# A streaming encoder step on one core: ties settled in a branch per tile, the sixteen rounds in a branch of their own, eleven gate tiles ahead of attention, and part of a convolution tile summed on VectorE

## The chip, the cores and the metric

The kernel runs on one core of a Trainium2 chip. The core has a matrix engine (TensorE, PE in the profile; PEld are its weight loads), VectorE (DVE), ScalarE (ACT), GpSimd (POOL) and a queue for DMA issues (SyncE, SP). Each engine works through its own instruction list in order and waits on semaphores for the others. The metric is the device time of one execution in microseconds (us), the median of several runs; lower is better.

## The reference

One layer of an encoder over 1024 prompt frames and 64 sample frames (1088 tokens, width 1024, float32). What the change touches is the selection of keys for attention and the causal convolution.

```
h = x + 0.5 * swiglu(rms(x));  u = rms(h);  z = u @ W_in
q, k, v, qi, ki, wi, conv_in, gate = split(z)
# indexer and selection
s     = einsum('bqhd,bsd->bqhs', qi, k_idx)
score = einsum('bqh,bqhs->bqs', wi, relu(s));  score = where(admissible, score, -inf)
_, sel = top_k(score, top)            # top = 256 (prompt) or 48 (sample); the lower index wins a tie
attn  = attention of q over the selected keys only
# convolution branch
c  = ca * sigmoid(cb)
dc = depthwise_conv(c_pad, conv_w, width 31) + conv_b      # 512 channels
conv_out = silu(layernorm(dc)) @ conv_w_out
# merge
g_a, g_c = sigmoid(gate + b_gate)
h = h + (g_a * (attn @ attn_w_out) + g_c * conv_out) @ w_out
h = h + 0.5 * swiglu(rms(h));  y = rms(h)
```

The inputs are drawn from a fixed seed, so each execution sees the same scores. Frame t may read the keys up to the end of its chunk of 64. Selection is needed only where more keys are admissible than are kept: six prompt tiles of 128 rows with 384, 512, 640, 768, 896 and 1024 keys, and the sample tile of 64 rows with 192 keys. That makes 832 rows and 4416 key columns in all.

## The kernel before, in words

**Stages.** First feed-forward block (PE, to about 780 us); a middle part with the projections of u, rotary, indexer, selection, attention, convolution and merge (about 780 to 1775 us); second feed-forward block (to the end). Every float32 matmul is done as three passes (`mm3`, L136 to L138) on operands that are split into a high and a low part: ACT makes the high part (`whi`), POOL the low part (`wlo`, L119).

**The middle part in program order.** `conv_in(t)` projects u and makes the gated convolution input of channel tile t in DRAM (`d_c`). `conv(t, ...)` loads it (`ci`), sums 31 shifted copies and stores the result (`d_dc`). For tiles 0, 1 and 2 ACT multiplies by the tap (`pd`, L679) and POOL adds (`ac`, L680), in two halves of 559 tokens; for tile 3 one DVE instruction a tap multiplies and adds (L665) in a PSUM bank, in three pieces. Then come rotary (`rope`, DVE), the indexer (matmuls into `lgi` PSUM banks, ACT relu, DVE weighting into the scores `Y`, L836/L838), the value projection, `conv(1)`, `conv(2)`, the query projection, and then the selection.

**The selection on DVE.** Scores are searched by bits. Fifteen rounds (L901) find the high 16 bits `hib` of each row's threshold. Then the eight largest low halves among the scores that share these high bits are taken (`top8`), the threshold's rank among them is `thr`, and if it is at most 7 the low half `lob` is read off; `nxt` becomes the difference to the next low half (L947). A mask is written to `bias` (L958: 0 for a kept key, a large negative number for others). If `nxt` is zero in any row (a tie, or a rank over 7, for which `lob` and `nxt` come out as zero), the flag `deepi` is set (L948 to L954), DVE loads it into a register (L961) and branches (L962). In that branch sixteen more rounds over all seven tiles (L973 to L983, the counting at L979) find the low half bit by bit, and then eight instructions a tile (L990 to L998) rank the tied keys and rewrite the mask of all seven tiles. The search's small arrays (`srch`, `sb_` in the code) lie in a PSUM bank of the pool `lgi`.

**After the selection.** Keys, values and queries of attention are loaded (`K`, `vt`, `qts`). The 16 gate tiles (`gates`, tanh of a projection of u, three chunks of 364, 362 and 362 tokens each, 24 matmuls a chunk) are split: the first `GPRE` = 10 run ahead of attention with the PSUM pool `ps4`; the rest are the first work of `background()`, which fills attention's gaps, in the pool `psf`, whose banks lie where `ps4` and `lgi` were. After the first ten, `cvs.close()`, `low.close()` and `ps_es.close()` free the convolution's and the search's memory, and attention's tiles (`pr`, `lg`, L1066 to L1083) are put there. `lg` scores queries against keys, L1069 adds the mask, and so on.

**What sets the order.** A scheduler orders each engine's instructions at build time, by priorities (`high_priority`) and its own estimates; at run time the lists are fixed. Nothing crosses a branch on DVE; the other engines have one plain jump there and no condition.

Of the kernel before, what the change touches and what calls it, by code (L numbers as in the profile page):

```python
# [54 lines left out]
CW = 31  # L55
# [12 lines left out]
STILES = [(128 * i, 128, 0, 128 * (i + 1), TOP_P) for i in range(2, 8)]  # L68
# [7 lines left out]
NT = len(STILES)  # L76
# [16 lines left out]
class Kern:  # L93
# [346 lines left out]
    def run(self):  # L440
        tc, nc, a = self.tc, self.nc, self.a
        PS = bass.MemoryType.PSUM
        with ExitStack() as top:
# [6 lines left out]
            d_c = dram.tile([4, P, 1148], F32, name="d_c")  # L450
            d_dc = dram.tile([4, P, 1118], F32, name="d_dc")
# [192 lines left out]
            lgi = self.pool(ps_es, "lgi", 4, space=PS)  # L644
# [7 lines left out]
            kp = self.pool(low, "topk", 1, side="right")  # L652
            Y = kp.tile([P, YCOLS], F32, name="Y")

            def conv(t, dve):
                x = "d" if dve else "p"
                if dve:
                    for s0, w in ((0, 374), (374, 372), (746, 372)):
                        ci = cvp_.tile([P, 589], F32, name="ci", tag="ci" + x)[:, :w + 30]
                        nc.sync.dma_start(ci, d_c[t, :, s0:s0 + w + 30])  # L660
                        ac = lgi.tile([P, 512], F32, name="acc", tag="lgi")[:, :w]
                        nc.scalar.activation(ac, ci[:, 0:w], AF.Identity, scale=par("convw", t * CW),
                                             bias=par("convb", t))
                        for j in range(1, CW):
                            nc.vector.scalar_tensor_tensor(ac, ci[:, j:j + w], par("convw", t * CW + j), ac,  # L665
                                                           op0=ALU.mult, op1=ALU.add)
                        co = cvp_.tile([P, 559], F32, name="ac", tag="ac" + x)[:, :w]
                        nc.scalar.activation(co, ac, AF.Copy)
                        nc.sync.dma_start(d_dc[t, :, s0:s0 + w], co)
                    return  # L670
                for s0 in (0, 559):
                    ci = cvp_.tile([P, 589], F32, name="ci", tag="ci" + x)
                    nc.sync.dma_start(ci, d_c[t, :, s0:s0 + 589])
                    ac = cvp_.tile([P, 559], F32, name="ac", tag="ac" + x)
                    nc.scalar.activation(ac, ci[:, 0:559], AF.Identity, scale=par("convw", t * CW),
                                         bias=par("convb", t))
                    for j in range(1, CW):
                        pd = cvp_.tile([P, 559], F32, name="pd", tag="pd", bufs=2)
                        nc.scalar.activation(pd, ci[:, j:j + 559], AF.Copy, scale=par("convw", t * CW + j))  # L679
                        nc.gpsimd.tensor_tensor(ac, ac, pd, op=ALU.add)  # L680
                    nc.sync.dma_start(d_dc[t, :, s0:s0 + 559], ac)

            def load_q(pool, src, t0, rows, qpool=None, qb=2, n=1280):

# [180 lines left out]
            conv(1, False)  # L865
            conv_in(2, ep)
            conv(2, False)

            rope_pairs(tb, d_q)
            tbs.close()  # L870
# [68 lines left out]
            def threshold():  # L939

                nc.vector.tensor_copy(mi0, hib)
                nc.vector.tensor_copy(mi1, lob)
                nc.vector.tensor_scalar(mi0, mi0, 16, None, op0=ALU.logical_shift_left)
                nc.vector.tensor_tensor(sth.bitcast(I32), mi0, mi1, op=ALU.bitwise_or)  # L944
# [4 lines left out]
            nc.vector.transpose(deep[:, 32:64], deep[:, 0:32])  # L949
            nc.vector.tensor_reduce(deep[:, 64:65], deep[:, 32:64], axis=AX.X, op=ALU.min)  # L950
            for q in range(1, 4):
                nc.vector.tensor_copy(deep[0:1, 64 + q:65 + q], deep[32 * q:32 * q + 1, 64:65])
            nc.vector.tensor_reduce(deep[0:1, 68:69], deep[0:1, 64:68], axis=AX.X, op=ALU.min)
            nc.vector.tensor_scalar(deepi, deep[0:1, 68:69], 0.5, None, op0=ALU.is_lt)  # L954
# [7 lines left out]
            with tc.If(more > 0):  # L962


                nc.vector.tensor_scalar(flag, hib, float(1 << 15), None, op0=ALU.is_lt)
                nc.vector.tensor_scalar(sgn, flag, 2.0, -1.0, op0=ALU.mult, op1=ALU.add)
                nc.vector.tensor_tensor(thr, ktop, lmk, op=ALU.subtract)
                nc.vector.tensor_tensor(thr, thr, flag, op=ALU.mult)
                nc.vector.tensor_tensor(thr, thr, lmk, op=ALU.add)
                nc.vector.memset(lob, 0.0)  # L970
                nc.vector.tensor_copy(low_, lob)
                for b in range(15, -1, -1):
                    nc.vector.tensor_scalar(lob, low_, float(1 << b), None, op0=ALU.add)  # L973
                    threshold()
                    nc.vector.tensor_tensor(cand, sth, sgn, op=ALU.mult)
                    for n in VT + (XT,):
                        rows, y0, L = rows_of(n)
                        c1 = slice(COL[n], COL[n] + 1)
                        nc.vector.scalar_tensor_tensor(spare(n), Y[:rows, y0:y0 + L], sgn[:rows, c1],  # L979
                                                       cand[:rows, c1].to_broadcast([rows, L]),  # L980
                                                       op0=ALU.mult, op1=ALU.is_ge, accum_out=cnt[:rows, c1])
                    nc.vector.tensor_tensor(flag, cnt, thr, op=ALU.is_ge)
                    nc.vector.scalar_tensor_tensor(low_, flag, float(1 << b), low_, op0=ALU.mult, op1=ALU.add)  # L983
                nc.vector.tensor_copy(lob, low_)
                threshold()
                for n in VT + (XT,):
                    rows, y0, L = rows_of(n)
                    c1 = slice(COL[n], COL[n] + 1)
                    y, b = Y[:rows, y0:y0 + L], spare(n)
                    nc.vector.tensor_scalar(b, y, sth[:rows, c1], 0.0, op0=ALU.is_le, op1=ALU.add,  # L990
                                            accum_out=cnt[:rows, c1])
                    nc.vector.tensor_scalar(need[:rows, c1], cnt[:rows, c1], float(STILES[n][4] - L), None, op0=ALU.add)
                    nc.vector.tensor_scalar(y, y, sth[:rows, c1], None, op0=ALU.is_equal)
                    nc.vector.tensor_tensor_scan(y, y, y, 0.0, op0=ALU.add, op1=ALU.bypass)
                    nc.vector.tensor_scalar(y, y, need[:rows, c1], -NEG, op0=ALU.min, op1=ALU.mult)
                    nc.vector.scalar_tensor_tensor(b[:, 0:1], b[:, 0:1], NEG, y[:, 0:1], op0=ALU.mult, op1=ALU.add)
                    nc.vector.tensor_tensor(y[:, 0:L - 1], y[:, 1:L], y[:, 0:L - 1], op=ALU.subtract)
                    nc.vector.scalar_tensor_tensor(b[:, 1:L], b[:, 1:L], NEG, y[:, 0:L - 1], op0=ALU.mult, op1=ALU.add)  # L998
# [504 lines left out]
```

## Time and profile before

| | us |
|---|---|
| median of 3 runs | 2552.09 (2544.73 to 2552.24) |
| profiled execution: its own time | 2549.7 |
| profiled execution: span from first to last instruction | 2547.9 |
| PE busy | 2316.0 (91%) |
| DVE busy | 1847.4 (73%) |
| POOL busy | 1435.6 (56%) |
| ACT busy | 1164.8 (46%) |
| mean granted TensorE clock | 0.959 |

The profiled execution is 1.8 us longer than its span, and 2.4 us shorter than the median of the runs. A row of a timeline gives start, duration, engine, line, operation, output<-inputs, shapes, number of merged instructions, and in brackets how long the engine had been idle and what ended that. Where several instructions are merged in one row, the duration is from the first start to the last end. Busy PE time is modelled from overlapping records; two consecutive starts give the true pace. `L979` is line 979 of the kernel before.

### The profile page before, as it was taken

Reading aid. Unit: us, or ns where it says so; the run is one execution under the profiler, and the core shown is the slowest. Engines: PE = TensorE matmul, PEld = TensorE weight load, DVE = VectorE, ACT = ScalarE, POOL = GpSimd, SP = SyncE. Lnnn points to the kernel's source line nnn. Section 1 sums busy time; section 2 is a strip of 40 time slices with the busy share of each in tenths; the row PEclk is TensorE's granted clock in tenths of the full one; section 3 lists DMA queues with packets and bytes.
Section 4 is the critical chain, followed back from the end, with each engine's and each line's share of the span. In section 5 each row is a group of like instructions: output and inputs, shape, how many; then the busy total and the mean of one; then the engine's idle time right before and its main releaser. Section 6 shows DMA issues by size and latency. Waiting matters only on the chain.

```text
span 2547.9 us, 44592 instructions
## 1 busy us (share of the span) xinstructions
PE 2316.0 (91%) x16762; PEld 2283.4 (90%) x16762; DVE 1847.4 (73%) x4138; ACT 1164.8 (46%) x2237; POOL 1435.6 (56%) x873
## 2 busy tenths in 40 slices
PE   7999999999999999993048989989999999999998
PEld 6999999999999999993048888979999999999998
DVE  7766678766673776899996788557776668767676
ACT  6433345443355568862014555444444345344343
POOL 5455566555466868796045345546555565555554
PEclk9999999999999999997569999989999999999999
DMA  5222323223234432331002245564222222323223
GB/s 181 109 96 96 108 100 118 84 92 108 91 114 137 138 118 87 124 125 46 0 23 68 85 154 164 185 218 144 100 100 92 84 100 84 105 105 118 90 93 110
DMA packets 130408, 273.46 MB, mean 107 GB/s; under 512 B 17936, under 2 KB 77200, under 8 KB 130192
## 3 DMA queue, kind: packets, MB, share of 16 engines
q1 hardware_dynamic: 130192, 270.61, 31.3%
q8 instruction: 132, 2.16, 0.3%
q14 instruction: 84, 0.69, 0.1%
HBM read 231.87 MB, written 38.75 MB: 106 GB/s over the span
## 4 chain that ended last, share of the span: by engine, by line
PE 71%; DVE 16%; DMA 4%; POOL 4%; issue 3%; ACT 2%; SPq 0%; DVEq 0%; ACTq 0%; POOLq 0%
PE ps L136 22%; PE ps L138 22%; PE ps L137 22%; DVE bias L979 4%; POOL ac L680 3%; DMA raw<-wf 1%; PE pt L1093 1%; DMA ga<-d_g 1%; DVE bias L901 1%; DVE ps L312 1%; DVE ga L1230 1%; PE ps L166 1%; DVE x L153 1%; DVE s L314 1%; DVE t L211 1%
## 5 line engine op out<-in xcount | busy, mean ns | idle before, releaser
L119 POOL TENSOR_TENSOR wlo<-raw,whi 128x1024 fp32r<-128x1024 f32 (+1 forms) x187 | 437.3, 2343 | 377.8 <-ACT whi L118 373.9
L136 PE MATMUL ps<-x,whi 128*128 128x272 f32 (+2 forms) x1544 | 484.5, 314 | 137.5 <-DVE sth L944 119.8
L136 PE MATMUL ps<-x,wp 128*128 128x272 f32 x1760 | 506.5, 289 | 3.2 <-ACT wp L152 3.2
L138 PE MATMUL ps<-x,wp 128*128 128x272 f32 x1760 | 503.6, 290 | 2.0 <-DVE wp L153 1.0
L137 PE MATMUL ps<-x,wp 128*128 128x272 f32 x1760 | 505.1, 288 | 0.0
L138 PE MATMUL ps<-x,wlo 128*128 128x272 f32 (+2 forms) x1544 | 481.9, 313 | 0.0
L136 PEld LDWEIGHTS ps<-x,whi 128*128 128x128 f32 x1544 | 294.4, 191 | 140.8 <-DVE sth L944 120.5
L137 PE MATMUL ps<-x,whi 128*128 128x272 f32 (+2 forms) x1334 | 413.7, 310 | 0.9 <-POOL x L153 0.9
L136 PE MATMUL ps<-gh,whi 128*128 128x272 f32 x1408 | 400.1, 289 | 5.6 <-DVE spare L284 3.5
L137 PE MATMUL ps<-gl,whi 128*128 128x272 f32 x1408 | 405.2, 289 | 0.0
L138 PE MATMUL ps<-gh,wlo 128*128 128x272 f32 x1408 | 404.2, 289 | 0.0
L680 POOL TENSOR_TENSOR ac<-ac,pd 128x559 f32<-128x559 f32 x180 | 287.0, 1595 | 157.7 <-ACT pd L679 132.3
L153 POOL TENSOR_TENSOR wlo<-raw,whi 128x1024 fp32r<-128x1024 f32 x88 | 221.4, 2517 | 256.2 <-ACT whi L152 256.2
L136 PEld LDWEIGHTS ps<-x,wp 128*128 128x128 f32 x1760 | 331.2, 188 | 4.2 <-ACT wp L152 4.0
L138 PEld LDWEIGHTS ps<-x,wp 128*128 128x128 f32 x1760 | 328.8, 188 | 3.9 <-DVE wp L153 2.7
L137 PEld LDWEIGHTS ps<-x,wp 128*128 128x128 f32 x1760 | 331.5, 188 | 0.0
L153 POOL TENSOR_TENSOR wp<-s,wp 128x512 fp32r<-128x512 f32 x176 | 256.6, 1458 | 103.3 <-ACT wp L152 103.3
L428 DVE SCALAR_TENSOR_TENSOR h<-ps,h 128x272 f32<-128x272 f32 x384 | 164.4, 438 | 186.9 <-PE ps L138 186.2
L138 PEld LDWEIGHTS ps<-x,wlo 128*128 128x128 f32 x1544 | 294.0, 191 | 1.2
L118 ACT ACTIVATE whi<-raw 128x1024 fp32r<-128x1024 f32 (+1 forms) x187 | 190.5, 1020 | 221.3 <-PE ps L137 110.3
L136 PEld LDWEIGHTS ps<-gh,whi 128*128 128x128 f32 x1408 | 263.5, 189 | 6.9 <-DVE spare L284 3.9
L138 PEld LDWEIGHTS ps<-gh,wlo 128*128 128x128 f32 x1408 | 266.3, 189 | 0.0
(264 smaller groups left out, 5035.6 us busy)
## 6 DMA issues: line engine op xcount, KB each, us to landing
raw<-wf SPq DMA_DIRECT2D x337, 512.0 KB, 3.3
raw<-wf SPq DMA_DIRECT2D x32, 384.0 KB, 3.0
d_g<-sg SPq DMA_DIRECT2D x32, 181.0 KB, 1.9
d_h<-h SPq DMA_DIRECT2D x2, 2176.0 KB, 10.5
y<-t SPq DMA_DIRECT2D x32, 136.0 KB, 1.9
raw<-d_q SPq DMA_DIRECT2D x32, 128.0 KB, 3.5
raw<-d_qi SPq DMA_DIRECT2D x24, 128.0 KB, 3.1
d_g<-sg SPq DMA_DIRECT2D x16, 182.0 KB, 3.3
```

What stands on the lines that cost most here:

```text
L118: nc.scalar.activation(hi[:, :n], raw[:, :n], AF.Copy)
L119: self.weng.tensor_tensor(lo[:, :n], raw[:, :n], hi[:, :n], op=ALU.subtract)
L136: t.matmul(out, wh, xh, start=first, stop=False)
L137: t.matmul(out, wh, xl, start=False, stop=False)
L138: t.matmul(out, wl, xh, start=False, stop=last)
L153: (eng or nc.vector).tensor_tensor(lo, x, hi, op=ALU.subtract)
L166: self.nc.tensor.matmul(ps[:, b * P:(b + 1) * P], x[:, t0:t0 + P], self.ones, start=i == 0, stop=i == len(tiles) - 1)
L211: self.nc.vector.scalar_tensor_tensor(x, h[:, k, t0:t0 + w], self.par[:, q:q + 1], r, op0=ALU.mult, op1=ALU.mult)
L312: nc.vector.tensor_tensor(s[2], a0, b0, op=ALU.subtract)
L428: nc.vector.scalar_tensor_tensor(x, p, 0.5, x, op0=ALU.mult, op1=ALU.add)
L680: nc.gpsimd.tensor_tensor(ac, ac, pd, op=ALU.add)
L979: nc.vector.scalar_tensor_tensor(spare(n), Y[:rows, y0:y0 + L], sgn[:rows, c1], cand[:rows, c1].to_broadcast([rows, L]), op0=ALU.mult, op1 ...
```

## The change

Four things are changed.

1. **Two branches where there was one.** In the outer branch DVE now computes one flag for each tile (a row of it is tied: `nxt` is zero) and one more flag `far` (a row's rank is over 7 and its eighth low half isn't zero), with a helper `flags()` that reduces over the partitions, and stores them in `tiei`. The sixteen rounds stand in a nested branch on `far`. If it isn't taken, the low half found before is used as it is.
2. **Ties in a branch per tile.** For each of the seven tiles DVE loads the tile's flag and branches over six instructions (before: eight, for every tile). The rank goes to an array `rk` of its own, and the mask that L962 (L958 before) has written is corrected by one instruction.
3. **`GPRE` is 11**: one more gate tile stands ahead of attention.
4. **Convolution tile 0 is split** at token 506: VectorE sums the first 506 tokens in a PSUM bank as tile 3 does, ACT and POOL the other 612 in one piece. Tile 3 keeps its three pieces, tiles 1 and 2 their two halves.

```diff
-GPRE = 10
+GPRE = 11
...
-            def conv(t, dve):
...
+            def conv(t, pieces):
+
+                for s0, w, dve in pieces:
+                    x = "d" if dve else "p"
+                    ci = cvp_.tile([P, 536 + 106 * (not dve)], F32, name="ci", tag="ci" + x)[:, :w + 30]
+                    nc.sync.dma_start(ci, d_c[t, :, s0:s0 + w + 30])
+                    co = cvp_.tile([P, 506 + 106 * (not dve)], F32, name="ac", tag="ac" + x)[:, :w]
+                    ac = lgi.tile([P, 512], F32, name="acc", tag="lgi")[:, :w] if dve else co
...
+                    for j in range(1, CW):
+                        if dve:
                             nc.vector.scalar_tensor_tensor(ac, ci[:, j:j + w], par("convw", t * CW + j), ac,
                                                            op0=ALU.mult, op1=ALU.add)
+                        else:
+                            pd = cvp_.tile([P, 612], F32, name="pd", tag="pd", bufs=2)[:, :w]
+                            nc.scalar.activation(pd, ci[:, j:j + w], AF.Copy, scale=par("convw", t * CW + j))
+                            nc.gpsimd.tensor_tensor(ac, ac, pd, op=ALU.add)
...
-            conv(0, False)
-            conv(3, True)
+            conv(0, ((0, 506, True), (506, 612, False)))
+            conv(3, ((0, 374, True), (374, 372, True), (746, 372, True)))
...
+            def flags(src, first, dst):
+
+                w = src.shape[1]
+                f = [deep[:, first + 32 * i:first + 32 * i + 32] for i in range(3)]
+                nc.vector.transpose(f[1], f[0])
+                nc.vector.tensor_reduce(f[2][:, 0:1], f[1], axis=AX.X, op=ALU.min)
+                for q in range(1, 4):
+                    nc.vector.tensor_copy(f[2][0:w, q:q + 1], f[2][32 * q:32 * q + w, 0:1])
+                nc.vector.tensor_reduce(f[0][0:w, 0:1], f[2][0:w, 0:4], axis=AX.X, op=ALU.min)
+                nc.vector.transpose(f[1][0:32, :], f[0][0:32, :])
+                nc.vector.tensor_scalar(dst, f[1][0:1, 0:w], 0.5, None, op0=ALU.is_lt)
...
             with tc.If(more > 0):
...
+                nc.vector.tensor_copy(deep[:, 0:NT], nxt)
+                nc.vector.tensor_scalar(flag, thr, 7.5, None, op0=ALU.is_ge)
+                nc.vector.tensor_tensor(flag, flag, top8[:, :, 7], op=ALU.mult)
+                nc.vector.tensor_reduce(deep[:, NT:NT + 1], flag, axis=AX.X, op=ALU.max)
+                nc.vector.tensor_scalar(deep[:, NT:NT + 1], deep[:, NT:NT + 1], -1.0, 1.0, op0=ALU.mult, op1=ALU.add)
+                flags(deep[:, 0:NT + 1], 0, tiei)
+                far = nc.vector.value_load(tiei[:, NT:NT + 1], min_val=0, max_val=1)
+                with tc.If(far > 0):
+
+                    nc.vector.memset(tiei, 1)
...
+                for n in (5, 6, 4, 3, 2, 1, 0):
                     rows, y0, L = rows_of(n)
...
+                    tied = nc.vector.value_load(tiei[:, c1], min_val=0, max_val=1)
+                    with tc.If(tied > 0):
+                        y, b = Y[:rows, y0:y0 + L], spare(n)
+                        nc.vector.tensor_scalar(y, y, sth[:rows, c1], 0.0, op0=ALU.is_equal, op1=ALU.add,
+                                                accum_out=need[:rows, c1])
+                        nc.vector.scalar_tensor_tensor(need[:rows, c1], cnt[:rows, c1], 1.0 / NEG, need[:rows, c1],
+                                                       op0=ALU.mult, op1=ALU.add)
+                        nc.vector.tensor_scalar(need[:rows, c1], need[:rows, c1], float(STILES[n][4] - L), None,
+                                                op0=ALU.add)
+                        nc.vector.tensor_tensor_scan(rk[:rows, :L], y, y, 0.0, op0=ALU.add, op1=ALU.bypass)
+                        nc.vector.scalar_tensor_tensor(y, rk[:rows, :L], need[:rows, c1], y,
+                                                       op0=ALU.is_gt, op1=ALU.mult)
+                        nc.vector.scalar_tensor_tensor(b, y, NEG, b, op0=ALU.mult, op1=ALU.add)
```

Where the sixteen rounds and the old tie code stood, the rounds are unchanged inside the nested branch, and end with a fresh mask (seven instructions like L958).

How the change moves instructions shows at three places. The first is PE's list at the step from the gate tiles that run ahead to attention: `ps` are gate chunks, `lg` attention's first scores, `x` and `u` parts of u, `whi`/`wlo` a gate tile's weights. Before:

```order
L138 MATMUL ps_14509<-x_9450,wlo_14449 128x362
L1066 MATMUL lg_14561<-kh0_13603,qt_13634 128x512
L1067 MATMUL lg_14561<-kl0_13604,qt_13634 128x512
L1066 MATMUL lg_14565<-kh0_13603,qt_13634 128x512
L1067 MATMUL lg_14565<-kl0_13604,qt_13634 128x512
L1066 MATMUL lg_14570<-kh0_13603,qt_13634 128x512
L1067 MATMUL lg_14570<-kl0_13604,qt_13634 128x512
L962 UNCONDITIONAL_BRANCH
L136 MATMUL ps_14636<-x_9443,whi_14631 128x364
L137 MATMUL ps_14636<-x_9451,whi_14631 128x364
```

And PE's list at the same place with the change (`ps_14631` is the last chunk of the eleventh gate tile):

```order
L136 MATMUL ps_14631<-x_9449,whi_14570 128x362
L966 UNCONDITIONAL_BRANCH
L137 MATMUL ps_14631<-u_9457,whi_14570 128x362
L138 MATMUL ps_14631<-x_9449,wlo_14571 128x362
L136 MATMUL ps_14631<-x_9450,whi_14570 128x362
L137 MATMUL ps_14631<-u_9457,whi_14570 128x362
L138 MATMUL ps_14631<-x_9450,wlo_14571 128x362
L1091 MATMUL lg_14683<-kh0_13635,qt_13666 128x512
L1092 MATMUL lg_14683<-kl0_13636,qt_13666 128x512
...
L1092 MATMUL lg_14692<-kl0_13636,qt_13666 128x512
L136 MATMUL ps_14758<-x_9443,whi_14753 128x364
```

The 72 matmuls of the eleventh gate tile now stand ahead of the first `lg`; behind the first six `lg` matmuls PE goes on with gate chunks in both, and meets the next `lg` matmul after 168 gate rows before and after 101 with the change.

The second place is DVE's list at the outer branch with the change, from the flag `deepi` on (before, `deepi` at L954 was followed by its load L961, the branch L962 and at once by L965, the first of the sixteen rounds' preparation):

```order
L955 TENSOR_SCALAR deepi<-srch 1x1
L965 TENSOR_LOAD deepi
L966 COMPARE_AND_BRANCH
L969 COPY srch<-nxt 128x7
...
L955 TENSOR_SCALAR tiei<-srch 1x8
L975 TENSOR_LOAD tiei
L976 COMPARE_AND_BRANCH
L978 MEMSET tiei 1x8
L979 TENSOR_SCALAR flag<-srch 128x7
```

And where the first of the seven tiles' branches stands, behind the nested branch:

```order
L1003 SCALAR_TENSOR_TENSOR bias,cnt<-Y,sth,negc 128x1024
L976 UNCONDITIONAL_BRANCH x2
L975 ISA x2
L1011 TENSOR_LOAD tiei
L1012 COMPARE_AND_BRANCH
L1014 TENSOR_SCALAR Y,need<-Y,sth 128x1024
L1016 SCALAR_TENSOR_TENSOR need<-cnt,need 128x1
L1020 SCALAR_TENSOR_TENSOR rk<-Y 128x1024
L1018 TENSOR_SCALAR need<-need 128x1
L1021 SCALAR_TENSOR_TENSOR Y<-rk,need,Y 128x1024
L1023 SCALAR_TENSOR_TENSOR bias<-Y,bias 128x1024
L1012 UNCONDITIONAL_BRANCH x2
```

Between the two pieces lie some 260 rows, the nested branch's, which DVE jumps over if `far` is not set; the last piece comes seven times, once a tile.

The third place is DVE's list at the convolution (`acc` is the PSUM bank, `sg` belongs to `conv_in(3)`, whose PSUM source `ps` PE is to reuse, `m0` and `m1` to rotary). Before and with the change:

```order
L623 SCALAR_TENSOR_TENSOR sg_10141<-sg_10141,ps_10195 128x364
L623 SCALAR_TENSOR_TENSOR sg_10168<-sg_10168,ps_10223 128x362
L665 SCALAR_TENSOR_TENSOR acc_10501<-ci_10499,par_72,acc_10501 128x374 x4
L623 SCALAR_TENSOR_TENSOR sg_10251<-sg_10251,ps_10278 128x362
L665 SCALAR_TENSOR_TENSOR acc_10501<-ci_10499,par_72,acc_10501 128x374 x4
L580 TENSOR_TENSOR m0_10696<-ps_10645,cos_10616 128x364
```

```order
L667 SCALAR_TENSOR_TENSOR acc_10312<-ci_10309,par_72,acc_10312 128x506 x14
L623 SCALAR_TENSOR_TENSOR sg_10141<-sg_10141,ps_10195 128x364
L667 SCALAR_TENSOR_TENSOR acc_10312<-ci_10309,par_72,acc_10312 128x506 x4
L623 SCALAR_TENSOR_TENSOR sg_10168<-sg_10168,ps_10223 128x362
L667 SCALAR_TENSOR_TENSOR acc_10312<-ci_10309,par_72,acc_10312 128x506 x9
L623 SCALAR_TENSOR_TENSOR sg_10251<-sg_10251,ps_10278 128x362
L667 SCALAR_TENSOR_TENSOR acc_10312<-ci_10309,par_72,acc_10312 128x506 x3
L580 TENSOR_TENSOR m0_10638<-ps_10587,cos_10558 128x364
L667 SCALAR_TENSOR_TENSOR acc_10444<-ci_10441,par_72,acc_10444 128x374 x2
```

Thirty sums of 506 columns stand among the evictions of `conv_in(3)`, and tile 3's sums of 374 columns come behind them.

More of the change, by code (lines that the diff above doesn't have):

```diff
@@ L653, in run @@
             Y = kp.tile([P, YCOLS], F32, name="Y")
-            def conv(t, dve):
[L656 to L664, printed above, removed]
+            def conv(t, pieces):
[5 more added lines that the diff above has]
+                    ac = lgi.tile([P, 512], F32, name="acc", tag="lgi")[:, :w] if dve else co
+                    nc.scalar.activation(ac, ci[:, 0:w], AF.Identity, scale=par("convw", t * CW),
+                                         bias=par("convb", t))
+                    for j in range(1, CW):
+                        if dve:
@@ L665, in conv @@
                             nc.vector.scalar_tensor_tensor(ac, ci[:, j:j + w], par("convw", t * CW + j), ac,
                                                            op0=ALU.mult, op1=ALU.add)
-                        co = cvp_.tile([P, 559], F32, name="ac", tag="ac" + x)[:, :w]
-                        nc.scalar.activation(co, ac, AF.Copy)
[L669 to L681, printed above, removed]
@@ L780, in run @@
             deepi = kp.tile([1, 1], I32, name="deepi")
+            tiei = kp.tile([1, NT + 1], I32, name="tiei")
+            rk = kp.tile([P, 1024], F32, name="rk")
             def cols(g):
@@ L864, in run @@
             conv_in(1, ep)
-            conv(1, False)
+            conv(1, ((0, 559, False), (559, 559, False)))
             conv_in(2, ep)
-            conv(2, False)
+            conv(2, ((0, 559, False), (559, 559, False)))
             rope_pairs(tb, d_q)
@@ L947, in run @@
             nc.vector.tensor_tensor(nxt, lob, nxt, op=ALU.subtract)
-            nc.vector.tensor_reduce(deep[:, 0:1], nxt, axis=AX.X, op=ALU.min)
[L949 to L954, printed above, removed]
+            def flags(src, first, dst):
[8 more added lines that the diff above has]
+                nc.vector.tensor_scalar(dst, f[1][0:1, 0:w], 0.5, None, op0=ALU.is_lt)
+            nc.vector.tensor_reduce(deep[:, 0:1], nxt, axis=AX.X, op=ALU.min)
+            flags(deep[:, 0:1], 0, deepi)
             for n in (5, 4, 6, 3, 2, 1, 0):
@@ new lines, in run @@
+                flags(deep[:, 0:NT + 1], 0, tiei)
+                far = nc.vector.value_load(tiei[:, NT:NT + 1], min_val=0, max_val=1)
+                with tc.If(far > 0):
+                    nc.vector.memset(tiei, 1)
+                    nc.vector.tensor_scalar(flag, hib, float(1 << 15), None, op0=ALU.is_lt)
+                    nc.vector.tensor_scalar(sgn, flag, 2.0, -1.0, op0=ALU.mult, op1=ALU.add)
+                    nc.vector.tensor_tensor(thr, ktop, lmk, op=ALU.subtract)
+                    nc.vector.tensor_tensor(thr, thr, flag, op=ALU.mult)
+                    nc.vector.tensor_tensor(thr, thr, lmk, op=ALU.add)
+                    nc.vector.memset(lob, 0.0)
+                    nc.vector.tensor_copy(low_, lob)
+                    for b in range(15, -1, -1):
+                        nc.vector.tensor_scalar(lob, low_, float(1 << b), None, op0=ALU.add)
+                        threshold()
+                        nc.vector.tensor_tensor(cand, sth, sgn, op=ALU.mult)
+                        for n in VT + (XT,):
+                            rows, y0, L = rows_of(n)
+                            c1 = slice(COL[n], COL[n] + 1)
+                            nc.vector.scalar_tensor_tensor(spare(n), Y[:rows, y0:y0 + L], sgn[:rows, c1],
+                                                           cand[:rows, c1].to_broadcast([rows, L]),
+                                                           op0=ALU.mult, op1=ALU.is_ge, accum_out=cnt[:rows, c1])
+                        nc.vector.tensor_tensor(flag, cnt, thr, op=ALU.is_ge)
+                        nc.vector.scalar_tensor_tensor(low_, flag, float(1 << b), low_, op0=ALU.mult, op1=ALU.add)
+                    nc.vector.tensor_copy(lob, low_)
@@ L978, in run @@
                         c1 = slice(COL[n], COL[n] + 1)
[L979 to L983, printed above, removed]
@@ L984, in run @@
-                nc.vector.tensor_copy(lob, low_)
-                threshold()
-                for n in VT + (XT,):
-                    rows, y0, L = rows_of(n)
[L988 to L998, printed above, removed]
+                        nc.vector.scalar_tensor_tensor(spare(n), Y[:rows, y0:y0 + L], sth[:rows, c1],
+                                                       negc[:rows].to_broadcast([rows, L]),
+                                                       op0=ALU.is_lt, op1=ALU.mult, accum_out=cnt[:rows, c1])
```

20 lines of the change are left out of this document (7 added, 13 removed).

## The prediction

> **What bounds the kernel now.** First the page's slices, 63.7 us each.
>
> ```profile
> PE   7999999999999999993048989989999999999998
> DVE  7766678766673776899996788557776668767676
> POOL 5455566555466868796045345546555565555554
> ```
>
> PE is the bound except in one hole, slices 18 to 20, where DVE alone is full. What fills the hole is in the group rows and the timeline of the search's branch:
>
> ```profile
> L136 PE MATMUL ps<-x,whi 128*128 128x272 f32 (+2 forms) x1544 | 484.5, 314 | 137.5 <-DVE sth L944 119.8
> 1180.00:1300.00 120.00, 1.83 (x5) 0.92 (x3) 115.37 (x343) 1.11 (x2) 8.27 (x4) 0.51 0.01 5
> 1173.75 0.14 DVE L954 TENSOR_SCALAR deepi<-srch 1x1 int32<-1x1 f32 x1
> 1174.95 0.17 DVE L965 TENSOR_SCALAR flag<-srch 128x7 f32<-128x7 f32 x1 [1.05 <-ACT pd L679]
> 1175.15 0.17 DVE L966 TENSOR_SCALAR sgn<-flag 128x7 f32<-128x7 f32 x1
> 1301.61 1.15 DVE L990 TENSOR_SCALAR_CACHE_REDUCE bias<-Y,sth 128x896 bf16<-128x896 f32 x1
> 1301.63 0.67 PE L136 MATMUL ps<-x,whi 128*128 128x364 f32 x1 [119.80 <-DVE sth L944]
> ```
>
> L965 runs, so the branch is taken, for these inputs, and the sixteen rounds last from 1175 to 1301.6 us. PE waits 119.8 us for the last `sth`, because its next gate chunk needs a PSUM bank that the search holds. The other two engines stop behind PE, and the way back into full work is longer than the rounds:
>
> ```profile
> 1308.93 19.80 POOL L680 TENSOR_TENSOR ac<-ac,pd 128x559 f32<-128x559 f32 x6 [120.50 <-ACT pd L679]
> 1331.21 15.45 POOL L680 TENSOR_TENSOR ac<-ac,pd 128x559 f32<-128x559 f32 x3
> 1340.29 5.14 DVE L998 SCALAR_TENSOR_TENSOR bias<-bias,Y 128x895 bf16<-128x895 bf16 x7
> 1346.68 0.32 SPq L681 DMA_DIRECT2D d_dc<-ac  x1
> 1348.87 1.06 ACT L691 ACTIVATE qt<-raw 128x1024 fp32r<-128x1024 f32 x1 [9.84 <-DMA d_dc<-ac]
> 1349.05 0.69 DVE L1069 CUSTOM_DVE_ANT_0 pr<-lg,bias 128x512 f32<-128x512 f32 x1 [3.61 <-POOL wlo L119]
> 1349.80 0.79 PE L1066 MATMUL lg<-kh,qt 128*128 128x512 f32 x1 [7.71 <-DVE mb L1069]
> 1360.00:1380.00 20.00, 20.00 (x130) 19.16 (x129) 11.60 (x27) 10.78 (x18) 9.42 (x4) 1.00 0.18 62
> ```
>
> Attention starts only when three lanes have arrived: DVE with the ties (to 1345.43), POOL with the last nine sums of `conv(2)` (to 1346.66, plus the store that frees the memory, 2.4 us to L1069), and PE with its gate chunks. Call R the start of the `lg` matmul at 1349.80. From there PE is full again (20.00 of 20), with the same work left before and after the change, so **the gain is 1349.8 minus the new R**.
>
> **What the inputs decide.** No profile shows whether `far` is set; the inputs do. I worked the scores out from the reference's seeded inputs, in float64 and rounded to float32 where the kernel rounds. Of 832 rows two have a tie at the threshold, both at score zero, in the tiles of 640 and of 1024 keys; the largest rank is 6 (two rows), and `far` needs 8. So two tile branches run, and the rounds don't, unless TensorE's rounding moves a row by two ranks.
>
> **DVE's lane.**
>
> ```profile
> 1167.75 0.33 PE L137 MATMUL ps<-u,whi 128*128 128x362 f32 x1
> 1167.91 0.32 PE L138 MATMUL ps<-x,wlo 128*128 128x362 f32 x1
> 1173.81 0.76 ACT L679 ACTIVATE pd<-ci,par 128x559 f32<-128x559 f32 x1 [3.63 <-POOL ac L680]
> 1172.48 0.22 DVE L949 STREAM_TRANSPOSE srch<-srch 128x32 f32<-128x32 f32 x1
> 1305.95 1.27 DVE L990 TENSOR_SCALAR_CACHE_REDUCE bias<-Y,sth 128x1024 bf16<-128x1024 f32 x1
> 1303.61 0.87 DVE L990 TENSOR_SCALAR_CACHE_REDUCE bias<-Y,sth 128x640 bf16<-128x640 f32 x1
> 1313.02 9.63 DVE L994 TENSOR_TENSOR_SCAN Y<-Y 128x896 f32<-128x896 f32 x7
> ```
>
> - Start: 1173.89, the end of L954. With the change 19 more projection matmuls stand ahead of the last indexer matmul on PE; at PE's pace of 0.166 us (1167.75 to 1167.91) that is 3.1. One more transposition and its step: 0.3. So 1177.3.
> - A branch: between L954's end and L965 lie 1.05, of which the ACT instruction named accounts for some: it ended at 1174.57, 0.38 earlier. So a load and branch costs 0.38 to 1.05. I take 1.05, nine times: 9.4. A jump over skipped code isn't in the trace; I take it as nothing, and price it below.
> - Flags: five small instructions at 0.20 (L965 to L966) and a reduction like L949 to L954 (1.41) with one more transposition: 2.7.
> - Tie bodies: compare 1.27, two small ones 0.4, scan 9.63 x 1024/4416 = 2.23, two more passes at 1.27: 6.4 for 1024 keys; for 640 likewise 0.87 + 0.4 + 1.40 + 1.74 = 4.4. Together 10.8.
>
> Sum 1177.3 + 9.4 + 2.7 + 10.8 = **1200**, where it was 1345.4.
>
> **POOL's lane.**
>
> ```profile
> 1140.47 10.23 POOL L680 TENSOR_TENSOR ac<-ac,pd 128x559 f32<-128x559 f32 x6 [1.06 <-ACT ac L675]
> 1150.66 2.98 POOL L119 TENSOR_TENSOR wlo<-raw,whi 128x1024 fp32r<-128x1024 f32 x1
> 1182.68 5.75 POOL L680 TENSOR_TENSOR ac<-ac,pd 128x559 f32<-128x559 f32 x3
> L680 POOL TENSOR_TENSOR ac<-ac,pd x180: 1362/1398/11476, 806.1 to 1335.2; 128x559 f32<-128x559 f32 x180
> 947.33 0.14 POOL L841 MEMSET Y<- 64x64 f32 x1 [16.67 <-DVE Y L838]
> 945.97 0.32 SPq L673 DMA_DIRECT2D ci<-d_c  x1
> ```
>
> The last half of `conv(2)` starts at 1140.47, and by 1188.43 has 21 of its 30 sums (6, 6, 6 and 3). Then ACT stands behind PE, and POOL behind ACT, for 120.5 us. Without that stop the nine go on at 10.23/6 = 1.70 us, with one `wlo` of 3.0: 1188.4 + 15.3 + 3.0 = 1206.7, and with the 2.4 for store and first mask **1209**. Convolution tile 0 asks about 38 us less of POOL (60 sums at the median of 1.40 become 30 of 612 columns, 1.53), but that buys nothing: POOL already waits 16.7 us here for `ci` of tile 1, which PE's projection delivers.
> These sums are stretched when DVE works beside them: the six from 1308.93 take 19.8 us, 8.4 at the median.
> [...]
>
> **PE's lane.**
>
> ```profile
> 1178.91 0.79 PE L1066 MATMUL lg<-kh,qt 128*128 128x512 f32 x1 [10.67 <-ACT sg L1019]
> 1179.50 0.63 PE L1067 MATMUL lg<-kl,qt 128*128 128x512 f32 x1
> 1179.93 0.63 PE L1066 MATMUL lg<-kh,qt 128*128 128x512 f32 x1
> ```
>
> The eleventh gate tile adds 72 matmuls, 12.0, to the last at 1167.9: 1180. The first `lg` follows 11.0 later, as now, because ACT's `sg` queues behind POOL-paced products: 1191. Six `lg` matmuls at 0.43 (1179.50 to 1179.93) are 2.6, then 101 gate rows 16.8, if no bank is waited for: **1210**. The search frees its bank when DVE has passed the inner branch, about 1182, so that wait is gone. The gate tile's own load, split and three stores move ahead on SP, ACT and POOL with it; they are the same in number and fill the hole.
>
> **The convolution on DVE.**
>
> ```profile
> 823.37 0.53 DVE L623 SCALAR_TENSOR_TENSOR sg<-sg,ps 128x364 f32<-128x364 f32 x1 [15.39 <-ACT ps L620]
> 827.32 0.53 DVE L623 SCALAR_TENSOR_TENSOR sg<-sg,ps 128x362 f32<-128x362 f32 x1 [3.42 <-ACT ps L620]
> 832.89 2.55 DVE L665 SCALAR_TENSOR_TENSOR acc<-ci,par,acc 128x374 f32<-128x374 f32 x4 [5.04 <-ACT acc L662]
> 839.01 0.54 DVE L580 TENSOR_TENSOR m<-ps,cos 128x364 f32<-128x364 f32 x1 [0.20 <-ACT wz L725]
> ```
>
> Four sums of 374 take 2.55, so 0.64 each; 132 more columns at 1.04 ns (the compares above: 0.40 for 384) give 0.78, and thirty 23.4. They fit: fourteen (10.9) into the 15.39 before the eviction at 823, four (3.1) into the 3.42 before 827, and nine and three (9.4) from 828 to the rotary row at 839, where tile 3's sums stand now. What is late next is tile 3: its first 374 sums wait for the input buffer that the thirty hold until 839, so for a load, and rotary's next rows, which free PE's banks, stand behind them on DVE. I put 1 us on that and hide it in PE's four banks. Bounds: 0 if the gaps hold, 23.4 on the search's start if none does.
>
> **Sum.** R is the latest lane, 1210 to 1211. Gain 1349.8 - 1211 = 139. 2549.7 - 139 = 2411, and 2.4 more on the scale of the median: **2413**.
>
> **Rivals.**
> - *Another lane is later*: jumps that cost, or POOL stretched as beside the old tie code. If each of six jumps over skipped code cost what a short store takes to land (2.2, from 1346.68 to 1348.87), DVE ends at 1213. If the nine sums kept the pace of the six from 1308.93 (3.3), R = 1188.4 + 29.7 + 3.0 + 2.4 = 1223; at that of the last three (15.45/3 = 5.15), 1240. Time 2416 to 2442. Against it: the stretch came beside 44 us of passes (1301.6 to 1345.4), of which 11 stay. Chance 0.19.
> [...]
> - *The convolution delays the search*: none of the gaps holds, 23 us on DVE's lane: R = 1224, time 2426. Against it: the gaps counted above. 0.08.
> - *More is gained*: ACT's `sg` doesn't lag, PE runs through: 1180 + 2.6 + 16.8 = 1200 and POOL keeps 1.4 a sum. Time 2400 to 2405. 0.08.
> - *Slower: `far` is set*, so the change doesn't do what it says. Then DVE's rounds stay (126.7 from L965 to L990), and a fresh mask comes, like a round's counting:
>
> ```profile
> 1192.06 5.67 DVE bias L979 x14
> ```
>
> That is 5.7; all seven bodies run (5.7 + 9.6 + 11.4 + 2.8 = 29.5), with branches and flags 12.1: 174 against 171.5 now, from a start 3.4 later. R is about 1356 and the time 2558, with 2.2 for each of the seven tiles' joins 2573. It decides with one row of 832 at rank 8. Against it: the largest rank is 6. 0.05, of which 0.01 at no price for the joins.
>
> **How the numbers follow.** Forecast 2413 (own range 2405 to 2421): 0.60. Range 2400 to 2442: it takes in both cases of a later lane and the one of more gain, and leaves out `far` and the tails. A measurement of this kernel tells about 0.3% (7.7 us) from no change; all cases but `far` lie far beyond it: faster 0.95, within 0.01, slower 0.04.
>
> **What would show it.** No DVE group like L979 with 112 counts; two groups of tie bodies, with 1024 and 640 keys; PE's idle before the gate chunk that waits for `sth` near zero instead of 119.8; PE's hole, now the 182 us from 1167.9 to 1349.8 with 30 us of gate chunks and `lg` in it (168 rows and 6), nearly filled; POOL without a 120 us gap; R near 1211, and the stretch from R to the end as long as now (1198 us). It is wrong if the rounds run, if R is released by DVE's ties or by a jump, or if the hole comes back in attention, whose background work is three steps shorter.

## The result, and the profile after

The changed kernel takes 2407.61 us (median of 4 runs, 2406.68 to 2412.01), the kernel before 2552.16 us in the runs beside it: a ratio of 0.9444, 95% interval 0.9423 to 0.9464 (ratios here and below are of the runs' means). The profiled execution took 2406.68 us, with a span of 2404.9 (2547.9 before) and a mean granted clock of 0.987 (0.959). The forecast was 2413.

The page of the changed kernel, its slices (60.1 us each now) and the projection's group:

```profile
PE   6999999999999999999798999699999999999998
DVE  7766767666668587689847886458666678676676
POOL 5455555555557563889943555357555555545554
L136 PE MATMUL ps<-x,whi 128*128 128x272 f32 (+2 forms) x1544 | 482.4, 313 | 8.1 <-ACT x L152 2.2
```

Slices 18 to 20, the hole, are gone but for a 7 in slice 19, and the idle time ahead of the projection's matmuls fell from 137.5 to 8.1 us: the 119.8 us that they waited for `sth` are no longer there. What is left of the hole stands in the timeline, engine by engine. First VectorE:

```profile
1174.97 0.15 DVE L955 TENSOR_SCALAR deepi<-srch 1x1 int32<-1x1 f32 x1
1176.16 0.17 DVE L969 COPY srch<-nxt 128x7 f32<-128x7 f32 x1 [1.05 <-ACT pd L671]
1178.69 0.15 DVE L955 TENSOR_SCALAR tiei<-srch 1x8 int32<-1x8 f32 x1
1183.35 1.28 DVE L1014 TENSOR_SCALAR_CACHE_REDUCE Y<-Y,sth 128x1024 f32<-128x1024 f32 x1 [4.50 <-DVEq L976]
1187.96 2.16 DVE L1021 SCALAR_TENSOR_TENSOR Y<-rk,need,Y 128x1024 f32<-128x1024 f32 x1
1190.16 2.28 DVE L1023 SCALAR_TENSOR_TENSOR bias<-Y,bias 128x1024 bf16<-128x1024 f32 x1
1195.57 0.88 DVE L1014 TENSOR_SCALAR_CACHE_REDUCE Y<-Y,sth 128x640 f32<-128x640 f32 x1 [3.13 <-DVEq L1012]
1200.68 1.91 DVE L1023 SCALAR_TENSOR_TENSOR bias<-Y,bias 128x640 bf16<-128x640 f32 x1
1209.17 0.69 DVE L1094 CUSTOM_DVE_ANT_0 pr<-lg,bias 128x512 f32<-128x512 f32 x1 [6.58 <-DMA d_dc<-ac]
```

The flags take from 1176.16 to 1178.84, then `far` is not set and the rounds don't run; two tie bodies run, 1024 and 640 keys. The 4.50 us in brackets are the nested branch and the first tile's branch together, the 3.13 are four tiles' branches (three jumped, then the tile's own). VectorE's last body ends at 1202.59; two more tiles are jumped, and the first mask of attention (L1094) then waits for something else, the store of `conv(2)`. POOL and its store:

```profile
1165.73 13.43 POOL L672 TENSOR_TENSOR ac<-ac,pd 128x559 f32<-128x559 f32 x6
1181.42 12.26 POOL L672 TENSOR_TENSOR ac<-ac,pd 128x559 f32<-128x559 f32 x6
1195.96 10.83 POOL L672 TENSOR_TENSOR ac<-ac,pd 128x559 f32<-128x559 f32 x6
...
1206.82 0.32 SPq L675 DMA_DIRECT2D d_dc<-ac  x1
```

The last sum ends at 1206.79, its store follows, and the mask starts at 1209.17. PE, the six early `lg` and the one that the prediction called R:

```profile
1191.28 0.80 PE L1091 MATMUL lg<-kh,qt 128*128 128x512 f32 x1 [13.07 <-ACT sg L1044]
1193.58 0.63 PE L1092 MATMUL lg<-kl,qt 128*128 128x512 f32 x1
1211.98 0.39 PE L1091 MATMUL lg<-kh,qt 128*128 128x512 f32 x1
```

Ahead of the first `lg` PE waits 13.07 us for `sg`, a gate chunk's output that ScalarE makes between the convolution's products. The row at 1211.98 has no bracket: PE had not waited. The first mask (1209.17, 0.69 long) had set its bank free at 1209.9, and PE was still busy with gate rows. So R = 1212.0, and PE's own lane is the last by 2 us. Against 1349.8 that is 137.8 us; the span fell by 143.0, so 5.2 came from behind R.

### The profile page after: what moved, and what is told of

The parts are those of the page before. It is cut to its first block, busy times and chain, and to the rows that moved or that the text cites. A ratio compares the mean times of both kernels' runs of the same rounds, so it can differ in the third digit from the quotient of the medians.

```text
span 2404.9 us, 44164 instructions
## 1 busy us (share of the span) xinstructions
PE 2301.6 (96%) x16762; PEld 2272.1 (94%) x16762; DVE 1713.3 (71%) x3769; ACT 1145.1 (48%) x2208; POOL 1379.0 (57%) x843
## 4 chain that ended last, share of the span: by engine, by line
PE 74%; DVE 10%; DMA 5%; POOL 4%; ACT 4%; issue 3%; SPq 0%; ACTq 0%; DVEq 0%; POOLq 0%
PE ps L136 23%; PE ps L138 23%; PE ps L137 23%; POOL ac L672 3%; DMA ga<-d_g 2%; DMA raw<-wf 1%; PE pt L1118 1%; PE ps L166 1%; DVE pr L1094 1%; DVE t L211 1%; DVE ps L312 1%; PE lg L1091 1%; ACT pd L671 1%; DVE pl L153 1%; POOL wlo L119 0%
## 5 line engine op out<-in xcount | busy, mean ns | idle before, releaser
L137 PEld LDWEIGHTS ps<-gl,whi 128*128 128x128 f32 x1408 | 266.2, 189 | 0.0
```

The costliest lines, as they stand in the source:

```text
L137: t.matmul(out, wh, xl, start=False, stop=False)
```

## The experiments

A table first, for the readings below: R is the start of the fourth `lg` matmul over `kh`, "left" the matmuls that the trace has from R to the end, good to one or two (54 of them are 9.0 us at PE's 0.166), and all is from the profiled executions except the medians.

| kernel | median | R | left | span | span - R |
|---|---|---|---|---|---|
| before | 2552.16 | 1349.8 | 8402 | 2547.9 | 1198.1 |
| changed | 2407.61 | 1212.0 | 8398 | 2404.9 | 1192.9 |
| changed, once more | 2406.97 | 1212.2 | 8398 | 2408.5 | 1196.3 |
| convolution back | 2406.79 | 1216.9 | 8403 | 2406.2 | 1189.3 |
| ten gate tiles | 2415.90 | 1208.9 | 8452 | 2411.3 | 1202.4 |
| branches alone | 2413.17 | 1213.1 | 8403 | 2412.1 | 1199.0 |
| `far` taken | 2553.39 | 1353.0 | 8397 | 2554.1 | 1201.1 |
| short jump | 2410.27 (one run) | 1212.1 | 8398 | 2408.5 | 1196.4 |
| 21 more branches | 2420.99 | 1223.2 | 8397 | 2425.1 | 1201.9 |
| twelve gate tiles | 2412.55 | 1215.2 | 8398 | 2412.7 | 1197.5 |
| tile 1 split too | 2421.18 | 1208.2 | 8475 | 2416.6 | 1208.4 |

### One part at a time: the convolution, the gate tile, the branches

```diff
-            conv(0, ((0, 506, True), (506, 612, False)))
+            conv(0, ((0, 559, False), (559, 559, False)))
```

> The changed kernel with convolution tile 0 as it was: two halves of 559 columns on ScalarE and GpSimd, no sums on VectorE. My theory: the 38 us that the change takes off GpSimd go into gaps (it waits for the input of tile 1), so nothing moves: the last sum of tile 2 ends near 1207, the first mask of attention starts near 1209, and the time is 2407 within 0.2%. Rival: GpSimd's lane needs the relief, and the last sums end up to 38 us later, near 1245: 2445.

Measured: 2406.79 us (2405.48 to 2409.63), ratio to before 0.9428 (0.9405 to 0.945). The time is as my theory had it; the place is not. GpSimd's last sum ends at 1212.8 and the first mask starts at 1215.5, 6 us later, not 38 and not 0. VectorE's lane is later too, by 4.4 us (its flag at 1183.07 instead of 1178.69). Ahead of both, PE had 5.4 us of gaps between 808 and 1175 where the changed kernel has 0.6, about as much:

```profile
808.00:1175.00 367.00, 361.64 (x2152) 357.35 (x2153) 282.16 (x603) 247.57 (x421) 305.00 (x198) 0.99 0.37 112
```
```profile
808.00:1175.00 367.00, 366.41 (x2192) 363.05 (x2191) 305.63 (x647) 229.69 (x395) 270.97 (x169) 1.00 0.36 113
```

These are two window rows, of this kernel and then of the changed one; the first number behind the length is PE's busy time, the fifth POOL's. What the split gives ahead of R, 4.9 us, is not in the time: behind R the changed kernel's execution is 3.6 us longer. So the split is worth nothing that can be measured.

```diff
-GPRE = 11
+GPRE = 10
```

> The changed kernel with ten gate tiles ahead of attention instead of eleven. My theory: the fourth lg matmul (1212.0 in the changed kernel) is then released by the first mask on VectorE, which waits for GpSimd's last sum, at about 1209.2 + 0.7 = 1210; the 72 matmuls of the gate tile (12.0 us) come later, when PE is full, so the time is about 10 us longer: 2417. Rival: the gate tile fills one of PE's gaps in attention (20 us lie idle between 1512 and 1562 in the changed kernel): the time stays at 2407, or falls by 2.

Measured: 2415.90 us (2413.08 to 2417.58), ratio 0.9465 (0.9444 to 0.9486). My theory of the time holds, and R is released by the first mask:

```profile
1208.18 0.69 DVE L1094 CUSTOM_DVE_ANT_0 pr<-lg,bias 128x512 f32<-128x512 f32 x1 [5.45 <-DMA d_g<-sg]
1208.93 0.50 PE L1091 MATMUL lg<-kh,qt 128*128 128x512 f32 x1 [0.76 <-DVE mb L1094]
```

Now PE's row has a bracket (`mb` is written by the instruction that adds the mask): PE arrived first and waited for the mask. The mask waited for a gate chunk's store (`d_g<-sg`), not for GpSimd, whose last sum had ended at 1205.4; so a fourth lane, the gate chunks' stores, lies close too. R is 3 us earlier with 54 matmuls more behind it. The eleventh tile is worth about 8 us here; R and the count give 6 of them.

Both undone together leave the branches alone:

> The kernel before with the branches alone: ten gate tiles, convolution tile 0 in two halves on GpSimd. My theory: nearly all of the gain is that of the rounds, 2417 (the ten gate tiles cost 10, the convolution nothing). Rival: the parts need each other, because GpSimd's lane sets the end of the hole without the relief: 2445 or more.

Measured: 2413.17 us (2408.85 to 2413.99), ratio 0.9447 (0.9424 to 0.947). My theory by the time, with the tile worth 6.4 here (2413.17 against 2406.79) and the convolution nothing. So of 144.6 us the branches give 139, the gate tile the rest. GpSimd's lane is the last in this kernel; its last sum ends at 1209.2:

```profile
1212.37 0.69 DVE L1094 CUSTOM_DVE_ANT_0 pr<-lg,bias 128x512 f32<-128x512 f32 x1 [9.76 <-DMA d_dc<-ac]
1213.12 0.50 PE L1091 MATMUL lg<-kh,qt 128*128 128x512 f32 x1 [1.50 <-DVE mb L1094]
```

The 6.4 us are not the hole's, though. This kernel and the one with the convolution back differ in the gate tile alone, and have the same 8403 matmuls behind R, with R 3.8 us earlier for ten tiles. The difference arises behind R, here with eleven tiles and then with ten:

```profile
1216.90:2406.20 1189.30, 1134.60 (x8403) 1113.93 (x8402) 824.69 (x1860) 539.48 (x1078) 623.31 (x351) 0.99 0.36 117
1213.12:2412.10 1198.98, 1144.08 (x8403) 1122.16 (x8403) 832.25 (x1862) 541.13 (x1081) 626.31 (x352) 0.98 0.37 116
```

The same matmuls keep PE busy for 9.5 us more, at a granted clock (the number behind the fifth busy time) of 0.98 instead of 0.99. The four runs of each agree: 0.983 to 0.986 over the whole execution with ten tiles, 0.986 to 0.988 with eleven. Why the clock goes with the tile is not shown.

### The rival that ends slower: `far` taken

```diff
-nc.vector.tensor_scalar(deep[:, NT:NT + 1], deep[:, NT:NT + 1], -1.0, 1.0, op0=ALU.mult, op1=ALU.add)
+nc.vector.tensor_scalar(deep[:, NT:NT + 1], deep[:, NT:NT + 1], 0.0, 0.0, op0=ALU.mult, op1=ALU.add)
```

> The changed kernel with the flag of the inner branch set always, so that the sixteen rounds run and all seven tie bodies follow them. By the prediction's rival 'far is set': the fourth lg matmul near 1356 and a time of 2558, or 2573 with 2.2 us for each tile's join. Rival: the rounds cost less than they did, since PE passes its join and works on beside them: up to 30 us less, 2530.

Measured: 2553.39 us (10 runs), ratio 1.0002 (0.9989 to 1.0015): as long as before.

```profile
1309.81 0.67 PE L136 MATMUL ps<-x,whi 128*128 128x364 f32 x1 [116.91 <-DVE sth L940]
1353.00 0.80 PE L1091 MATMUL lg<-kh,qt 128*128 128x512 f32 x1 [23.76 <-DVE mb L1094]
```

The old wait is back, with the old releaser. R is 1353, 3 us earlier than priced, and the 2.2 us that the rival put on each tile's join (the end of its branch) don't show: between the tie bodies VectorE is idle for at most 0.61. With the rounds back, the time is back: it had gone with them.

### What a branch costs, and which lane is last

The sixteen rounds and the fresh mask are taken out of the nested branch, and one memset stays in it:

```diff
                 with tc.If(far > 0):
                     nc.vector.memset(tiei, 1)
-                    nc.vector.tensor_scalar(flag, hib, float(1 << 15), None, op0=ALU.is_lt)
...
```

> The changed kernel with the sixteen rounds and the fresh mask left out of the inner branch: what stands between the inner branch and its join is one small instruction, so that the jump over it is short. It is not taken for these inputs, so the work done is the same. My theory: what the inner branch costs beyond a tile's branch is the length of its jump. The wait of 4.50 us ahead of the compare over 1024 columns (inner branch and first tile branch together) falls to two loads and branches, 1.6; VectorE's lane ends 2.9 us earlier, near 1201; GpSimd and PE end later than that anyway, so the time is 2407 within 5. Rival: the length doesn't matter and the 4.5 us are the load's and the flags': the wait stays 4.5.

Measured (one run): 2410.27 us.

```profile
1178.98 1.28 DVE L986 TENSOR_SCALAR_CACHE_REDUCE Y<-Y,sth 128x1024 f32<-128x1024 f32 x1 [1.59 <-DVEq L976]
1191.33 0.88 DVE L986 TENSOR_SCALAR_CACHE_REDUCE Y<-Y,sth 128x640 f32<-128x640 f32 x1 [3.22 <-DVEq L984]
```

L986 is the changed kernel's L1014. Its wait is 1.59 us instead of 4.50, the other 3.22 for 3.13: between these two traces the length of the jump costs 2.9 us (2.6 against the kernel with tile 1 split, where the same two branches with the long jump take 4.2). VectorE's compare comes 4.4 us earlier than in the changed kernel (2.9 of it from the jump, the rest from an earlier start), but R stays at 1212.1: VectorE's lane is not the last one.

```diff
+                    for _ in range(3):
+                        again = nc.vector.value_load(tiei[:, NT:NT + 1], min_val=0, max_val=1)
+                        with tc.If(again > 0):
+                            nc.vector.tensor_copy(cnt[:rows, c1], cnt[:rows, c1])
                     tied = nc.vector.value_load(tiei[:, c1], min_val=0, max_val=1)
```

> The changed kernel with 21 more loads and branches, three ahead of each tile's own; none is taken, each jumps over one small instruction. My theory: a load and a jump over a short body cost 0.78 us each (3.13 for four in the changed kernel), 16.4 in all, so VectorE's lane ends near 1220 instead of 1204 and becomes the latest: the first mask starts near 1220 to 1221 instead of 1209.2, the fourth lg matmul near 1222, and the time is 2416, less what attention's gaps take up (up to 6). [...]

Measured: 2420.99 us (2419.94 to 2426.92), ratio 0.949 (0.9474 to 0.9505).

```profile
1209.32 0.88 DVE L1018 TENSOR_SCALAR_CACHE_REDUCE Y<-Y,sth 128x640 f32<-128x640 f32 x1 [15.26 <-DVEq L1013]
...
1222.44 0.69 DVE L1098 CUSTOM_DVE_ANT_0 pr<-lg,bias 128x512 f32<-128x512 f32 x1 [8.81 <-issue]
```
```profile
1223.20 0.80 PE L1095 MATMUL lg<-kh,qt 128*128 128x512 f32 x1 [15.79 <-DVE mb L1098]
```

Sixteen loads and branches take 15.26, eight take 8.81: 0.95 to 1.10 each, more than my 0.78. Now VectorE's lane is the last, R is 1223.2, and 11.2 us on R become 13.4 in the time. VectorE's lane comes 18 us later than the changed kernel's 1204, and R 11.2; so VectorE had about 7 us to spare there, 5 of them ahead of GpSimd's store, and seven tiles' branches fit.

```diff
-            conv(1, ((0, 559, False), (559, 559, False)))
+            conv(1, ((0, 506, True), (506, 612, False)))
```

> The changed kernel with convolution tile 1 cut like tile 0 (506 columns summed on VectorE, 612 on GpSimd). The thirty sums of 0.78 us stand on VectorE between the masks of the indexer and the counts of the search, where it has no gaps of that size. My theory: VectorE's lane ends up to 23 us later, near 1222, GpSimd's earlier, and the time is 2407 + 10 to 18: this is the rival 'the convolution delays the search' made true. Rival: GpSimd's relief lets ScalarE's gate work run ahead and closes the 13 us gap ahead of the first lg matmul: 2395 to 2400.

Measured: 2421.18 us (2418.34 to 2429.85), ratio 0.9503 (0.9481 to 0.9525). The size is the one I expected, the way is another, and the rival is half right. GpSimd is done at 1149.7, and PE's wait ahead of the first `lg` does shrink:

```profile
1175.24 0.50 PE L1091 MATMUL lg<-kh,qt 128*128 128x512 f32 x1 [1.44 <-ACT sg L1044]
1190.47 0.67 PE L136 MATMUL ps<-x,whi 128*128 128x364 f32 x1 [13.57 <-DVEq L976]
1208.24 0.80 PE L1091 MATMUL lg<-kh,qt 128*128 128x512 f32 x1 [12.18 <-DVE mb L1094]
```

1.44 instead of 13.07. But PE only runs into the next two waits sooner: for the bank that the search holds until VectorE has passed the nested branch, and for the first mask. The search starts 8 us later (its flag at 1183.2 instead of 1175.0), not 23. VectorE's lane ends no later than 1207.5: no GpSimd sum runs beside its tie bodies (from 1190 to 1208.24 GpSimd is busy 0.00 us), and they are short:

```profile
L1021 DVE SCALAR_TENSOR_TENSOR Y<-rk,need,Y 128x1024 f32<-128x1024 f32 x1 | 1.3, 1284 | 0.0
L1023 DVE SCALAR_TENSOR_TENSOR bias<-Y,bias 128x1024 bf16<-128x1024 f32 x1 | 1.2, 1224 | 0.0
L1021 DVE SCALAR_TENSOR_TENSOR Y<-rk,need,Y 128x640 f32<-128x640 f32 x1 | 0.9, 883 | 0.0
```

(group rows: busy time, and mean ns of one). R is early, but 8475 matmuls stand behind it, 77 more, 13 us: the table's columns have to be read together.

### One more gate tile, and a load moved

GPRE = 12 in place of 11:

> The changed kernel with twelve gate tiles ahead of attention. My theory: from eleven on PE's own lane is the latest, so 72 more matmuls ahead of the fourth lg make it 12.0 us later (1224) with 72 fewer left behind it: the time is 2407 within 5. Rival 1: the gap of 13 us ahead of the first lg matmul is filled as well, 2395 to 2400. Rival 2: the tile is missed as filler in attention, 2412 to 2419.

Measured: 2412.55 us (2408.54 to 2414.5), ratio 0.9453 (0.9437 to 0.9468): just outside what I expected, at the low end of rival 2. R is 1215.2, not 1224, with the same 8398 matmuls behind it: the tile's rows stand ahead of the first `lg`, which waits 15.61 us for `sg` now, and 72 fewer gate rows stand between that and R. Rival 1 is out. Nothing is to be had from a twelfth tile; R gives 3 of its 5 us, and whether the rest is lost in attention isn't settled.

Last, PE waits 12.9 us for a `ga` (a gate, loaded back for the merge) near 1550, while the loads of `h` for the last part stand on SP's queue. One of the three was moved behind the first merge steps, beside the changed kernel once more:

```diff
-            for c0, w in CHUNKS[::-1]:
+            for c0, w in CHUNKS[:0:-1]:
...
+            c0, w = CHUNKS[0]
+            for i, _ in enumerate(merge(0, mp_)):
                 next(rest, None)
+                if 1 <= i <= 4:
+                    m = 2 * i - 2
+                    nc.sync.dma_start(h[:, m:m + 2, c0:c0 + w], d_h[:, m:m + 2, c0:c0 + w])
```

> The changed kernel with the load of h for the first 364 tokens, in four pieces, behind the first merge steps of that chunk instead of together with the loads of the other two chunks. In the changed kernel the three loads of 1.5 MB stand ahead of the gates' loads (ga) on SP's queue near 1540, and PE waits 12.9 us there for one ga. My theory: with a third of the bytes out of the way this wait falls by about 4, and the time to 2403 beside the changed kernel's 2407. Rival: the wait is that of the whole chain behind attention, and the time stays within 2 of the changed kernel's.

> The changed kernel itself once more, beside the next run on the same chip. My theory: 2407 within 3; the fourth lg matmul at 1212 within 1.

Measured: 2408.44 us (5 runs, ratio 0.9434, 0.941 to 0.9457) against 2406.97 (5 runs, ratio 0.9429, 0.9406 to 0.9452). No gain, and the longest wait for `ga` is 13.9 us, against 12.9 and 11.8 in the two traces of the changed kernel: my theory of that gap falls. What sets it stays open. None of the kernels here is measurably faster than the changed one.

## Why the prediction was right, point by point

- **What bounds**: R is the latest of three lanes, and each was made to show itself: VectorE's with 21 more branches (bracket `DVE mb`, R 1223), PE's with ten gate tiles (without its rows R is released by the mask), GpSimd's with the branches alone (the mask waits for its store, and R for the mask). The lanes are not independent: PE's contains a wait for ScalarE's `sg`, which stands behind GpSimd's sums and shrinks from 13.07 to 1.44 us once GpSimd is done early. And there is a fourth: with ten tiles a gate chunk's store was the last to arrive, which the prediction didn't list. R came to 1212.0 for 1211, and in the changed kernel PE was the last, then GpSimd 2 us ahead, then VectorE.
- **GpSimd's lane**: forecast 1206.7 and 1209, measured 1206.79 and 1209.17. The sums weren't stretched to 3.3 us: the last twelve took 12.26 + 10.83, 1.92 each for the 1.70 forecast, and a shorter `wlo` (2.4 for 3.0) and an earlier start made up for it. So the stretch was 2.7 us on twelve sums; more of it fell on VectorE, 5.5 us.
- **PE's lane**: forecast `lg` at 1191 and R at 1210, measured 1191.28 and 1211.98. The 101 gate rows took 18.0 us for 16.8: the first nine behind the wait came 0.30 apart, the others 0.166.
- **VectorE's lane**: forecast 1200, measured 1202.6 for the last body and two jumps more, about 1204 by my estimate (0.78 each, from the 3.13 for four). Two terms were mis-sized; R doesn't show it because this lane isn't the last. The tie bodies were priced at 6.4 and 4.4 from compares with nothing beside them, and took 9.1 (1183.35 to 1192.44) and 7.0 (1195.57 to 1202.59); with GpSimd idle (0.00 us busy), in the kernel with tile 1 split, they took 6.3 and 4.3. So the price was right for a VectorE alone, and the stretch that I looked for on GpSimd fell on VectorE. The profile of before already had it: its first round counts beside GpSimd's `wlo` and sums (1179.52 to 1188.43), its second alone.

```profile
1180.44 3.10 DVE L979 SCALAR_TENSOR_TENSOR bias<-Y,sgn,cand 128x768 bf16<-128x768 f32 x1
1193.13 1.01 DVE L979 SCALAR_TENSOR_TENSOR bias<-Y,sgn,cand 128x768 bf16<-128x768 f32 x1
```

  The start was 1175.1 for 1177.3; PE's gaps from 808 to 1168, 1.2 us before and 0.6 now, give 0.6 of these 2.2 us, and the rest is not shown.
- **Branches**: nine at 1.05 were 9.4. They came as 1.05, 4.50 for two and about 0.8 for each of the other six (3.13 for four; the last two are taken alike): 10.3. The jump over the rounds that I took as nothing costs 2.9 (4.50 against 1.59 with the short jump), the short ones less than I took here, though 0.95 to 1.10 each in the kernel with 21 more.
- **The convolution**: that it fits in the gaps and buys nothing is right by the time. The reason was right for GpSimd (of the 60 us from 880 to 940 it is busy 10.61, where it was 46.98), but the split did close gaps of PE ahead of the search, 5 us that the sum doesn't have and most of which the stretch behind R took back.
- **From R to the end**: forecast 1198, measured 1192.9, and 1196.3 once more. The count was right, 8402 before and 8398 after, but not its time: PE was busy 1143.5 us for it before, 1132.1 and 1136.0 in the two executions of the changed kernel, and waited 6 us more. The other kernels with as many matmuls behind R have 1196.4 to 1201.9, so 3.4 of the 5.2 us were that one execution. This term is known to some 5 us only; it is most of the difference between 2413 and 2407.6.
- **The gate tile** filled the hole as said where the convolution is split: 54 matmuls fewer are left, for 3 us on R. Without the split R and the count gain nothing by it. The runs put 6 to 8 us on it, which the prediction hadn't priced; without the split all of that lies behind R and goes with a higher granted clock, for which it had no term.

## What to carry to other kernels

A hole is worth its length less the next lane: list every engine that must arrive, with its own end, and compare their spread with what the change may add to each; here three lanes lay within 8 us, so 21 cheap branches already cost 13. A stage that starts earlier can be no gain at all if what stands behind it is only moved, so read R together with the work that is left. Taking the rounds out of the way of inputs that don't need them pays as long as those inputs don't come: with `far` set the kernel is as long as before (2553.39 us against 2552.09 beside it).

## What was not expected of the hardware

- **The longer jump took longer.** A load of a flag and a branch over a few instructions took 0.70 to 1.10 us on VectorE (2.8 for four in the kernel with tile 1 split, 3.13 for four in the changed kernel, 8.81 for eight with 21 more); with the jump over the rounds' some 260 instructions the wait was 2.9 us longer (4.50 against 1.59). With `far` taken, where no branch of the tiles jumps, VectorE is idle for at most 0.61 us between the tie bodies. What takes the 2.9 us is not shown. In the changed kernel's wait of 4.50 us (1178.84 to 1183.35) the DMA view counts one packet on a queue that it calls `instruction`:

```profile
q1 hardware_dynamic: 339, 0.58, 40.0%
q14 instruction: 1, 0.01, 0.8%
```

  In the 3.13 us of four short branches (1192.44 to 1195.57) it counts one as well, so the two waits don't differ in this.
- **VectorE's passes were longer too beside GpSimd's sums.** L1021 over 640 keys took 1.79 us beside them in the changed kernel and 0.88 in the kernel with tile 1 split, where GpSimd was idle; a pass over one column (L1016) took 0.88 to 1.01 and 0.16, while the scan over 1024 keys (L1020) took 2.28 in both. In the prediction I let only GpSimd's sums stretch.
